# Two tiles of x loaded, rounded and split in halves instead of whole, in the first pass of a hybrid attention and gMLP block

## The chip, the cores and the metric

The kernel runs on one core of one Trainium2 chip. The metric is the device time of one execution in microseconds (us), as the median of several runs. The engines are TensorE (PE, the matmuls), VectorE (DVE), ScalarE (ACT), GpSimd (POOL) and SyncE (SP, whose queue issues most DMA transfers). Each engine runs its own instructions in a fixed order and waits on semaphores for what it needs from the others. Of the granted clock that the profile lists for TensorE, 1.00 is full speed.

## What is computed

One layer of an encoder block for 1024 tokens of width 1024, in float32. All projections of the normalised stream share one weight matrix.

```python
h = rmsnorm(x, norm_gain)
z = jnp.einsum('bsd,de->bse', h, w_in)
q, k, v, gate_a, u_in, v_in, gate_b, g_merge = jnp.split(z, IN_SPLITS, axis=-1)
...
q = axial_rope(rmsnorm(q.reshape(B, S, N_Q_HEADS, HEAD_DIM), q_gain), row_ang, col_ang)
k = axial_rope(rmsnorm(k.reshape(B, S, N_KV_HEADS, HEAD_DIM), k_gain), row_ang, col_ang)
attn = block_attention(q, k, v) * jax.nn.silu(gate_a)
y_a = jnp.einsum('bse,ed->bsd', attn, w_proj_attn)
...
v_mix = jnp.einsum('gij,bcjgd->bcigd', w_spatial, vv) + b_spatial.T[:, :, None]
gm = u * v_mix.reshape(B, S, GMLP_WIDTH) * jax.nn.silu(gate_b)
y_b = jnp.einsum('bse,ed->bsd', gm, w_proj_gmlp)
g = jax.nn.sigmoid(g_merge.reshape(B, S, N_BRANCHES, D_MODEL) + b_merge)
y = g[:, :, 0, :] * y_a + g[:, :, 1, :] * y_b
return x + jnp.einsum('bsd,de->bse', y, w_out)
```

There are 8 query heads on 2 key and value heads of 64, and a final RMS norm behind the layer.

## The kernel before

**Numbers in two parts.** To keep float32 accuracy with faster matmuls, an operand is split into a rounded high part and a low part, the rest. A product is then three matmuls (`mm3`, L173 to L176): high by high (L174), high by low of the second operand (L175), low by high (L176). The high part of x is made on ACT with the norm gain as a scale (`xh`, L158), the low part on DVE from the raw tile and the high part (`xl`, L159). Weights get theirs in `split` (high L112, low L118).

**The first pass.** x comes in transposed, in 8 tiles (dt = 0 to 7) of 128 channels by 1024 tokens, each 512 KB. `load_x(dt)` cuts a tile along the tokens: it issues one DMA for each cut on SP's queue (L152), then one ACT and one DVE instruction for each. For dt = 0 there are three cuts (256, 256 and 512 tokens), for all others one of 1024. `first_w` (L144) brings the first key and value weights in two pieces of 256 columns between those of dt 0; the later ones come by `stream_w` in pieces of 128 by 512, each for two dt (the first of them, for dt 2 and 3, is `wh_175`, `wl_176` in the order). For each dt, 24 matmuls of 128 x 256 go into the two key and value accumulators `kv_89` (tokens 0 to 511) and `kv_90` (tokens 512 to 1023), eight token blocks of three. The scheduler puts some of `kv_90`'s L174 and L175 ahead of `kv_89`'s first L176.

**Then** follow the gate and value projections from natural weights (`nat_weights`, `nat_group`), keys, queries, and from about 140 us attention. There, `scores` makes one tile of scores s (L552, L553), its row-maximum nm on DVE (L555), the exponential P on ACT (L559), the normalised high part of p on ACT (L565) and the low part on DVE (L566), and then transposes p by DMA on SP's queue (L569). `mix` multiplies the transposed T with the values (o, L577); ACT copies half of o (L580) and DVE adds it into `og` (L584). Between the heads stand matmuls of the gates and of u (`ga`, `u`; `fill_a`, `fill_u`, L490 to L492), whose results DVE takes out of PSUM (`ga01w`, L496; `uw`, L513). Query tiles are rotated on DVE (`qst`, `qtmp`: L317 to L332), transposed on PE (`qtp`, L351) and copied by ACT (`qT`, L353).

**The g stage**, from about 450 us: the merge gates are made by seven products of sub-matrices. The weights of each (`graw`) get a common scale: ACT sums their squares (`gsq`, L820), PE adds up (`usg`, L675), ACT copies (`scg`, L677), POOL makes the scale (L678, L679), and ACT writes scaled weights (`wg`, L686), which the first matmul g (L174) reads. `xf`, `xfT`, `gk`, `gf`, `gfT` are high parts of the other operands (L112) and `y` copies out of PSUM (L639), all on ACT.

**What sets the order.** No order is written by hand. The framework's scheduler (L1039, with a simulated timeline) places every instruction of every engine by its own estimate of when its inputs are ready. An edit at the start therefore also changes the order far behind it. SP has eight DMA semaphores: each DMA issue waits for the eighth before it.

Of the kernel before, what the change touches and what calls it, by code (L numbers as in the profile page):

```python
# [30 lines left out]
def hybrid_block_kernel(  # L31
# [21 lines left out]
    def t4(tag, name, dt=F32, shape=(P, 1024)):  # L53
        return sb.tile(list(shape), dt, tag=tag, bufs=BUFS[tag], name=name)
# [28 lines left out]
    def H(h):  # L83
        return slice(512 * h, 512 * h + 512)

    def C(c):
        return slice(128 * c, 128 * c + 128)
# [55 lines left out]
    def first_w(j):  # L143
        nc.sync.dma_start(out=wr[:, 256 * j:256 * j + 256], in_=wall[W_KV, :, 256 * j:256 * j + 256])  # L144

    def load_x(dt):
        raw = t4("T16", f"xraw{dt}")
        hi = t4("xh", f"xh{dt}", F32R)
        lo = t4("xl", f"xl{dt}", F32R)
        cuts = [slice(0, 256), slice(256, 512), H(1)] if dt == 0 else [slice(0, 1024)]  # L150
        for i, r in enumerate(cuts):
            nc.sync.dma_start(out=raw[:, r], in_=xT[C(dt), r])  # L152
            if dt == 0 and i == 0:
                nc.scalar.dma_start(out=cs, in_=cst[:, 0:C_BSP])
            if dt == 0 and i != 1:
                first_w(i // 2)
        for r in cuts:
            act.activation(hi[:, r], raw[:, r], AF.Copy, scale=gain[:, dt:dt + 1])  # L158
            dve.scalar_tensor_tensor(out=lo[:, r], in0=raw[:, r], scalar=gain[:, dt:dt + 1], in1=hi[:, r].bitcast(F32),  # L159
                                     op0=ALU.mult, op1=ALU.subtract)  # L160
        xh.append(hi)
        xl.append(lo)
        return raw
# [16 lines left out]
    for i in range(4):  # L180
        for j in range(2):
            dt = 2 * i + j
            if dt == 0:
                wh = sb.tile([P, 512], F32R, tag="wh", bufs=3, name="whk0")
                wl = sb.tile([P, 512], F32R, tag="wl", bufs=3, name="wlk0")
                wr = sb.tile([P, 512], F32, tag="wraw", bufs=4, name="wrawk0")
            raw = load_x(dt)
            if i == 0:
                r = slice(256 * j, 256 * j + 256)
                split(wh[:, r], wl[:, r], wr[:, r], act)  # L190
            elif j == 0:
                wh, wl = stream_w(W_KV + i // 2, i % 2, act)
            r = slice(256 * j, 256 * j + 256)
            for tt in range(NT):
                o = kvb[tt // 2][:, 256 * (tt % 2):256 * (tt % 2) + 256]
                mm3(o, xh[dt][:, C(tt)], xl[dt][:, C(tt)], wh[:, r], wl[:, r],
                    dt == 0 and tt % 2 == 0, dt == 7 and tt % 2 == 1)
# [845 lines left out]
```

## Time and profile before

| | us |
|---|---|
| median of 3 runs | 745.79 (744.92 to 745.86) |
| the profiled execution | 745.8 |
| its span in the trace | 744.0 |
| PE busy | 716.9 (96%) |
| DVE busy | 595.9 (80%) |
| ACT busy | 446.2 (60%) |
| mean granted clock of PE | 0.988 |

Lines of the profile name a source line (L158), an engine, an operation and its tiles, output first (`xh<-xraw,cs`). Numbers behind tile names, as in `xh_136`, count allocations; since the change allocates more tiles, they differ by 3 to 6 between the two kernels for the same thing (`wh_175` before is `wh_181` now, `xh_168` is `xh_171`). Times in the trace are from the start of the span. In brackets at a row's end stands how long the engine idled before it, and what ended that.

### The profile page before, as it was taken

How to read it: one execution, taken by the hardware profiler on the slowest of the kernel's cores; microseconds unless marked ns; L12 is line 12 of the kernel's file. 1: busy time of each engine (PE TensorE's matmuls, PEld its weight loads, DVE VectorE, ACT ScalarE, POOL GpSimd, SP SyncE). 2: the span in 40 equal slices, each digit the busy share in tenths (PEclk: the TensorE clock that was granted, in tenths of full speed). 3: DMA queues.
4: the chain of work that ended last, by engine and by line, in shares of the span. 5: the costliest groups of instructions: out<-in, count | busy, mean ns of one | idle time of the engine just before them, and what ended most of it. 6: DMA issues, size and time to landing. Idle time of an engine off the chain costs nothing.

```text
span 744.0 us, 9918 instructions
## 1 busy us (share of the span) xinstructions
PE 716.9 (96%) x3609; PEld 536.4 (72%) x3609; DVE 595.9 (80%) x900; ACT 446.2 (60%) x783; POOL 105.5 (14%) x101
## 2 busy tenths in 40 slices
PE   8999999988899999999999996999999999999996
PEld 7978888767778888888877883555464556478885
DVE  5567988799898999988899999988887898962223
ACT  5645665576788898877787477655455446531011
POOL 0010232123122322232200002101101110000000
PEclk9999999999999999999999997999999999999999
DMA  8831301064769898898999800130031004440202
GB/s 312 296 100 36 114 15 42 1 117 96 139 129 169 175 175 144 156 180 160 162 231 330 180 26 1 56 128 15 3 139 57 0 1 156 160 166 1 113 29 85
DMA packets 152609, 85.47 MB, mean 115 GB/s; under 512 B 135408, under 2 KB 136048, under 8 KB 152560
## 3 DMA queue, kind: packets, MB, share of 16 engines
q1 hardware_dynamic: 152272, 84.56, 45.6%
q8 instruction: 28, 0.46, 0.2%
q10 hardware_dynamic: 288, 0.28, 0.1%
q14 instruction: 21, 0.17, 0.1%
HBM read 47.07 MB, written 4.19 MB: 69 GB/s over the span
## 4 chain that ended last, share of the span: by engine, by line
PE 82%; DVE 6%; DMA 5%; ACT 3%; issue 2%; POOL 1%; SPq 0%; POOLq 0%; ACTq 0%; DVEq 0%
PE o L577 6%; DMA T<-p 4%; PE out L175 4%; PE out L176 4%; PE out L174 4%; PE g L174 3%; PE g L175 3%; PE g L176 3%; PE s L552 3%; PE s L553 3%; PE q L174 2%; PE q L176 2%; PE v L174 2%; PE v L175 2%; PE q L175 2%; PE v L176 2%
## 5 line engine op out<-in xcount | busy, mean ns | idle before, releaser
L566 DVE SCALAR_TENSOR_TENSOR p<-P,ri,p 128x1024 f16<-128x1024 f32 x64 | 88.9, 1394 | 14.4 <-ACT p L565 14.0
L559 ACT ACTIVATE P<-s,nm 128x1024 f32<-128x1024 f32 x64 | 71.4, 1116 | 22.5 <-DVE nm L555 11.2
L565 ACT ACTIVATE p<-P,ri 128x1024 f16<-128x1024 f32 x64 | 72.9, 1143 | 15.3 <-DMA T<-p 12.0
L555 DVE TENSOR_REDUCE nm<-s 128x1 f32<-128x1024 f32 x64 | 77.8, 1217 | 4.5 <-PE s L553 4.1
L577 PE MATMUL o<-T,vS 128*128 128x256 f16 x512 | 61.8, 273 | 2.1 <-DMA T<-p 2.1
L577 PEld LDWEIGHTS <-vS 128*128 128x128 f16 x512 | 47.4, 98 | 15.9 <-issue 6.3
L552 PE MATMUL s<-kT,qT 128*128 128x512 f32 x128 | 52.9, 414 | 1.3 <-ACT P L559 1.3
L118 POOL TENSOR_TENSOR wl<-wraw,wh 128x512 fp32r<-128x512 f32 x24 | 36.0, 1504 | 110.2 <-ACT wh L112 94.7
L553 PE MATMUL s<-kT,qT 128*128 128x512 f32 x128 | 50.5, 395 | 0.0
L973 DVE TENSOR_TENSOR xr<-out,xr 128x1024 f32<-128x1024 f32 x7 | 8.6, 1225 | 47.9 <-PE out L176 47.8
L915 ACT ACTIVATE sq<-xr 128x1024 f32<-128x1024 f32 x7 | 7.4, 1062 | 65.4 <-DVE xr L973 65.4
L678 POOL TENSOR_SCALAR scg<-scg 128x1 f32<-128x1 f32 x8 | 5.4, 674 | 216.5 <-ACT scg L677 216.5
L112 ACT CAST wh<-wraw 128x512 fp32r<-128x512 f32 x35 | 21.5, 614 | 19.3 <-PE yb L175 7.5
L490 PE MATMUL ga<-xh,wh 128*128 128x512 f32 x64 | 26.0, 407 | 3.8 <-DVE uw L513 3.4
L552 PEld LDWEIGHTS s<-kT,qT 128*128 128x128 f32 x128 | 24.1, 188 | 6.7 <-ACT P L559 1.8
L553 PEld LDWEIGHTS s<-kT,qT 128*128 128x128 f32 x128 | 24.1, 188 | 4.9 <-issue 0.2
L686 ACT ACTIVATE wg<-graw,scg 128x512 f16<-128x512 f32 x16 | 11.4, 721 | 26.1 <-PE g L176 13.1
L490 PE MATMUL u<-xh,wh 128*128 128x512 f32 x64 | 25.5, 399 | 0.7 <-DVE ga01w L496 0.7
L492 PE MATMUL ga<-xh,wl 128*128 128x512 f32 x64 | 25.6, 400 | 0.0
L491 PE MATMUL ga<-xl,wh 128*128 128x512 f32 x64 | 25.5, 399 | 0.0
L176 PE MATMUL yb<-gmh,wl 128*128 128x512 f32 x64 | 25.5, 398 | 0.0
L174 PE MATMUL yb<-gmh,wh 128*128 128x512 f32 x64 | 25.2, 396 | 0.3 <-ACT gmh L112 0.3
(558 smaller groups left out, 2188.3 us busy)
## 6 DMA issues: line engine op xcount, KB each, us to landing
wraw<-in_wall_dram SPq DMA_DIRECT2D x59, 256.0 KB, 3.2
graw<-in_wall_dram SPq DMA_DIRECT2D x16, 512.0 KB, 4.5
xraw<-in_xT_dram SPq DMA_DIRECT2D x15, 512.0 KB, 7.8
xn<-in_x_dram SPq DMA_DIRECT2D x8, 512.0 KB, 6.6
wor<-in_wall_dram SPq DMA_DIRECT2D x8, 512.0 KB, 5.5
xr<-in_x_dram SPq DMA_DIRECT2D x8, 512.0 KB, 4.1
out_dram<-xr SPq DMA_DIRECT2D x7, 512.0 KB, 2.6
T<-p SPq DMA_TRANSPOSE x64, 4.7
```

The lines of the kernel that those rows point to most:

```text
L118: eng_lo.tensor_tensor(out=lo, in0=raw, in1=hi if hi.dtype == F16 else hi.bitcast(F32), op=ALU.subtract)
L174: pe.matmul(o, ah, bh, start=start, stop=False)
L175: pe.matmul(o, ah, bl, start=False, stop=False)
L176: pe.matmul(o, al, bh, start=False, stop=stop)
L490: pe.matmul(o, wh[:, C(dt % 4)], xh[dt][:, H(h)], start=(dt == 0), stop=False)
L552: pe.matmul(sp[:, H(hf)], qs, kT[:, 2 * v, H(hf)], start=True, stop=False)
L553: pe.matmul(sp[:, H(hf)], qs, kT[:, 2 * v + 1, H(hf)], start=False, stop=True)
L555: dve.tensor_reduce(out=nm, in_=sp, axis=AX.X, op=ALU.max, negate=True)
L559: act.activation(Pt, sp, AF.Exp, bias=nm, accum_out=rsum)
L565: act.activation(hi, Pt, AF.Copy, scale=ri)
L566: dve.scalar_tensor_tensor(out=lo, in0=Pt, scalar=ri, in1=hi, op0=ALU.mult, op1=ALU.subtract)
L577: pe.matmul(ot[:, 0:256], vS[:, kt, v, :], T[:, :, 8 * p + kt, :], start=(kt == 0 and p == 0), stop=(kt == 7 and p == 1))
```

## The change

dt 1 and dt 2 are cut in two halves of 512 tokens. `H(0)` and `H(1)` are the column slices 0 to 511 and 512 to 1023.

```diff
-        cuts = [slice(0, 256), slice(256, 512), H(1)] if dt == 0 else [slice(0, 1024)]
+        cuts = [slice(0, 256), slice(256, 512), H(1)] if dt == 0 else [H(0), H(1)] if dt < 3 else [slice(0, 1024)]
         for i, r in enumerate(cuts):
             nc.sync.dma_start(out=raw[:, r], in_=xT[C(dt), r])
...
         for r in cuts:
             act.activation(hi[:, r], raw[:, r], AF.Copy, scale=gain[:, dt:dt + 1])
             dve.scalar_tensor_tensor(out=lo[:, r], in0=raw[:, r], scalar=gain[:, dt:dt + 1], in1=hi[:, r].bitcast(F32),
                                      op0=ALU.mult, op1=ALU.subtract)
```

So each of the two tiles has two DMAs of 256 KB, two ACT and two DVE instructions of 128 x 512 where it had one of each. On SP, the halves of dt 1 and dt 2 stand one behind the other where the whole tiles stood, and dt 4's tile has moved ahead of two weight pieces. On PE, all matmuls of dt 0 and dt 1 keep their order, and the first changes stand at dt 4.

**VectorE at the start**, from the last low part of the first weights on (`xl_137` belongs to dt 1, `xl_169` and now `xl_172` to dt 2, `wl_176` and `wl_182` to the weights of dt 2 and 3; `gsc` and `gs` are small scales that no matmul of this pass reads). Before:

```order
L118 TENSOR_TENSOR wlk_92<-wrawk_93,whk_91 128x256
L240 TENSOR_SCALAR gsc<-ssx 128x1
L242 RECIPROCAL gsc<-gsc 128x1
L243 TENSOR_SCALAR gs<-cs,gsc 128x8
L159 SCALAR_TENSOR_TENSOR xl_137<-xraw_135,cs,xh_136 128x1024
L159 SCALAR_TENSOR_TENSOR xl_169<-xraw_167,cs,xh_168 128x1024
L118 TENSOR_TENSOR wl_176<-wraw_173,wh_175 128x512
L159 SCALAR_TENSOR_TENSOR xl_205<-xraw_203,cs,xh_204 128x1024
```

With the change:

```order
L118 TENSOR_TENSOR wlk_92<-wrawk_93,whk_91 128x256
L159 SCALAR_TENSOR_TENSOR xl_137<-xraw_135,cs,xh_136 128x512
L240 TENSOR_SCALAR gsc<-ssx 128x1
L159 SCALAR_TENSOR_TENSOR xl_137<-xraw_135,cs,xh_136 128x512
L242 RECIPROCAL gsc<-gsc 128x1
L159 SCALAR_TENSOR_TENSOR xl_172<-xraw_170,cs,xh_171 128x512
L243 TENSOR_SCALAR gs<-cs,gsc 128x8
L159 SCALAR_TENSOR_TENSOR xl_172<-xraw_170,cs,xh_171 128x512
L118 TENSOR_TENSOR wl_182<-wraw_179,wh_181 128x512
L159 SCALAR_TENSOR_TENSOR xl_211<-xraw_209,cs,xh_210 128x1024
```

The three small instructions stood ahead of the low parts; now they stand between the halves.

**VectorE in attention**, at about 174 to 187 us of the profile. `p_1620`, `p_1637` are the low parts of two heads, now `p_1626`, `p_1643`; `nm_1669` and `nm_1686` are row-maxima of the next two, now `nm_1675`, `nm_1692`. Before:

```order
L317 TENSOR_TENSOR qst_1373<-qst_1373,qf_1778 128x1024
L555 TENSOR_REDUCE nm_1669<-s_1664 128x1
L328 TENSOR_TENSOR qtmp_1776<-qst_1373,tabq 128x16x16 x4
L566 SCALAR_TENSOR_TENSOR p_1620<-P_1614,ri_1617,p_1620 128x1024
L562 RECIPROCAL ri_1634<-ri_1634 128x1
L331 TENSOR_TENSOR qst_1373<-qst_1373,tabq 128x1024
L584 TENSOR_TENSOR og_1661<-o_1699,o_1716 64x128 x2
L555 TENSOR_REDUCE nm_1686<-s_1681 128x1
L332 TENSOR_TENSOR qst_1373<-qst_1373,qtmp_1776 128x1024
L566 SCALAR_TENSOR_TENSOR p_1637<-P_1631,ri_1634,p_1637 128x1024
L562 RECIPROCAL ri_1674<-ri_1674 128x1
L496 TENSOR_TENSOR ga01w<-ga_2147,rB 128x512
```

With the change:

```order
L317 TENSOR_TENSOR qst_1379<-qst_1379,qf_1784 128x1024
L566 SCALAR_TENSOR_TENSOR p_1626<-P_1620,ri_1623,p_1626 128x1024
L328 TENSOR_TENSOR qtmp_1782<-qst_1379,tabq 128x16x16 x4
L562 RECIPROCAL ri_1640<-ri_1640 128x1
L555 TENSOR_REDUCE nm_1675<-s_1670 128x1
L331 TENSOR_TENSOR qst_1379<-qst_1379,tabq 128x1024
L566 SCALAR_TENSOR_TENSOR p_1643<-P_1637,ri_1640,p_1643 128x1024
L332 TENSOR_TENSOR qst_1379<-qst_1379,qtmp_1782 128x1024
L555 TENSOR_REDUCE nm_1692<-s_1687 128x1
L584 TENSOR_TENSOR og_1667<-o_1705,o_1722 64x128 x2
L562 RECIPROCAL ri_1680<-ri_1680 128x1
L496 TENSOR_TENSOR ga01w<-ga_2153,rB 128x512
```

The first p stands ahead of a row-maximum and the four qtmp now, the second ahead of L332, a row-maximum and the og pair, and the `ga01w` behind them has the same instructions ahead of it. On PE, near the same place, 18 matmuls of `ga` (15 of `ga_2147`, now `ga_2153`, and three of dt 5) have moved ahead of the four matmuls of the s that `nm_1669` reads. On ACT, a P and a p now stand between the first and the second pair of the next qT copies.

**ScalarE ahead of the first g matmul**, at about 449 to 456 us (`scg` is the copy on which POOL's scale and then `wg` wait). Before:

```order
L639 COPY y_4203<-yb_4548 128x1024
L112 CAST gk<-gat_3891 128x1024
L820 ACTIVATE gsq_4738,gss_4737<-graw_4734 128x512
L677 COPY scg_4597<-usg_4592 128x1
L112 CAST gf_4925<-gat_3891 128x1024
L112 CAST xfT_4270<-xraw_4210 128x512
L820 ACTIVATE gsq_4740,gss_4737<-graw_4734 128x512
L686 ACTIVATE wg_4611<-graw_4580,scg_4597 128x512
```

With the change:

```order
L112 CAST xfT_4276<-xraw_4218 128x512
L112 CAST gf_4931<-gat_3897 128x1024
L820 ACTIVATE gsq_4746,gss_4743<-graw_4740 128x512
L639 COPY y_4209<-yb_4554 128x1024
L112 CAST gk<-gat_3897 128x1024
L112 CAST xfT_4276<-xraw_4216 128x512
L677 COPY scg_4603<-usg_4598 128x1
L820 ACTIVATE gsq_4748,gss_4743<-graw_4740 128x512
L820 ACTIVATE gsq_4750,gss_4743<-graw_4740 128x512
L686 ACTIVATE wg_4617<-graw_4586,scg_4603 128x512
```

`gf`, one `xfT` and one `gsq` have moved from behind the L677 to ahead of it. One `xf` cast has moved ahead of the last L580 copy before this place, and on PE the o matmuls that this copy reads stand five matmuls earlier.

## The prediction

> **What bounds the kernel now.** I read the page first, its busy shares and its chain.
>
> ```profile
> span 744.0 us, 9918 instructions
> PE 716.9 (96%) x3609; PEld 536.4 (72%) x3609; DVE 595.9 (80%) x900; ACT 446.2 (60%) x783; POOL 105.5 (14%) x101
> ...
> PE 82%; DVE 6%; DMA 5%; ACT 3%; issue 2%; POOL 1%; SPq 0%; POOLq 0%; ACTq 0%; DVEq 0%
> ```
>
> TensorE (PE) is busy 96% of the span and makes 82% of the chain. Work on another engine is free unless PE waits for it, so an edit can only win or lose inside PE's waits, 744.0 − 716.9 = 27 us with the head and the tail. The list of PE's waits says where they are (waited for, then total, times, longest).
>
> ```profile
> PE g L174 <- ACT wg L686: 6.6, 1, 6.6
> PE ga L490 <- DVE uw L513: 3.4, 1, 3.4
> PE o L577 <- DMA T<-p: 2.1, 3, 1.4
> PE kv L174 <- ACT xh L158: 2.0, 1, 2.0
> PE qtp L351 <- ACT qT L353: 1.3, 1, 1.3
> PE u L490 <- DVE ga01w L496: 0.7, 1, 0.7
> PE kv L176 <- DVE xl L159: 0.6, 1, 0.6
> ```
>
> The two kv rows belong to the edited place. The chain of waits from 3 us on, and the granted clock by microsecond, show what they cost (window, length, busy time and count of PE, PEld, DVE, ACT, POOL, then PEclk, DMA share, GB/s).
>
> ```profile
> 3.05 6.40 DMA xraw<-in_xT_dram
> 9.48 1.16 ACT xh L158
> 10.66 1.29 DVE xl L159
> 12.00 0.47 PE kv L176
> ...
> 13.11 0.21 PE kv L174
> ...
> 15.92 0.12 PE kv L175
> ```
>
> ```profile
> 8.00:9.00 1.00, 0.70 (x6) 0.50 (x5) 0.29 (x2) 0.00 (x0) 0.47 (x1) 1.00 1.01 385
> ...
> 13.00:14.00 1.00, 1.00 (x7) 1.00 (x7) 0.91 (x3) 1.00 (x2) 0.00 (x0) 0.50 1.05 410
> ```
>
> The second tile of x (dt = 1) is one 512 KB load. It lands at 3.05 + 6.40 = 9.45. Its rounding on ScalarE (ACT) and its low part on VectorE (DVE) follow one behind the other, and TensorE's first L176 of dt = 1 starts at 12.00. From there a matmul comes every 0.21 us, at a granted clock of 0.50, and only at 15.9 every 0.12 us again. So the place costs two waits (2.0 + 0.6) and a slow stretch: 20 of dt 1's 24 matmuls lie behind 12.00, and 20 × 0.12 = 2.4 would have done where they took from 12.00 to 15.99, 1.6 us more. The trace shows no cause for the low clock but these waits.
>
> **Part A, the start.** Moved and added: two loads of 512 KB become four of 256 KB, two ACT and two DVE instructions become four each; no matmul changes.
>
> ```profile
> xraw<-in_xT_dram SPq DMA_DIRECT2D x1, 256.0 KB, 3.5
> DMA to landing us min/median/max: 3.4/3.8/4.3
> ```
> ```profile
> 6.36 0.75 DVE L159 SCALAR_TENSOR_TENSOR xl<-xraw,cs,xh 128x512 fp32r<-128x512 f32 x1 [0.38 <-ACT xh L158]
> ...
> 13.15 0.68 DVE L118 TENSOR_TENSOR wl<-wraw,wh 128x512 fp32r<-128x512 f32 x1
> ```
> ```profile
> 3.75 0.51 ACT L158 ACTIVATE xh<-xraw,cs 128x256 fp32r<-128x256 f32 x1 [1.10 <-DMA cs<-in_cst_dram]
> ...
> 4.95 1.37 ACT L158 ACTIVATE xh<-xraw,cs 128x256 fp32r<-128x256 f32 x2
> 11.82 0.60 ACT L112 CAST wh<-wraw 128x512 fp32r<-128x512 f32 x1
> ```
> ```profile
> 15.99 0.40 PE L174 MATMUL kv<-wh,xh 128*128 128x256 f32 x2
> ```
>
> Landing of the first half: the DMA engines are full from 8 us on, at 385 to 410 GB/s, so 256 KB take 0.65 us. Earliest: right behind the last piece in front of it, the second half of the first weights (issued at 2.58, landing 4.3 later, 6.9), that is 7.5. Latest: with the second half, 9.45. I take 8.8, 0.65 before the landing that the trace shows, the nearest row. ACT's half costs 0.60 (the cast of 128x512) to 0.86 (1.37 for a 256 and a 512 piece, less 0.51 for the 256); I take 0.7: 9.5. DVE's half costs 0.75: 10.3. TensorE's third matmul of dt 1 reads the second half (landed 9.45, rounded 10.2), so its first L176 comes at 10.35, not 12.00. At full clock the 20 matmuls end at 12.75; the second low part, at 11.1, is ready before they reach it.
>
> Then the low part of dt 2's weights decides. DVE's queue is now: half, L240, half, L242, half, L243, half, L118. The dt 2 halves start at about 11.2 and 12.0 and end at 12.85 (dt 2's tile lands 1.3 behind dt 1's, at 10.75, its second half is rounded by 11.5, and the weights' cast of 0.60 behind it ends by 12.2); the L118 (0.68) ends at 13.5. So the first L175 of dt 2 comes at 13.55. Before, two L174 start at 15.99 and 16.11 and the L175 at 16.23. **Gain 2.7 us**. Ends: 3.2 if TensorE sets the pace (12.75 + 0.24 = 13.0); 1.6 if the clock still drops (10.35 + 20 × 0.21 = 14.55, and 0.24); 0.9 if the halves land together and the clock drops.
>
> Two more issues stand on SP's queue, 0.47 us each, in front of every later load; the full DMA engines, not the issue, set those landings, so I cost them nothing. If that cover were gone, TensorE would come 2.7 early to a load that is 0.94 late, and A would be +0.9 in place of −2.7.
>
> Whether the gain lasts is read from the stretch behind.
>
> ```profile
> 16.00:142.00 126.00, 126.00 (x683) 108.00 (x682) 96.02 (x171) 74.98 (x125) 22.28 (x15) 1.00 0.29 98
> ```
> ```profile
> 168.59 1.23 DVE L555 TENSOR_REDUCE nm<-s 128x1 f32<-128x1024 f32 x1 [1.88 <-PE s L553]
> ```
>
> TensorE has no wait between 16 and 142 us, and DVE still waits for PE behind the busy stretch, at 168.59, so the chain moves up as a whole.
>
> Two rules of the Trainium skill speak here. "TensorE: Matmul & The Clock Gate", Part 1 (the HAM clock gate), says that the clock halves after an idle window of about 3.4 us; this trace shows half clock after waits of 2.0 and 0.6 with four matmuls between, so a literal reading of single gaps does not hold here, and by it the 1.6 us would not have been lost. "DMA: Bandwidth & Descriptors", in Anatomy of one DMA, gives each transfer a fixed 2.0 us, and in Bandwidth advises batches of 1 MiB: it speaks against the change; were the fixed part paid one after another, two more transfers would bring dt 2's last half 4 us later, and the time to about 746, an estimate from that page. No row here shows transfers of the full queue paying it in turn, since 385 to 410 GB/s leaves no gap; it is rival 4.
>
> **Part B, attention from 163 to 200 us.** The order is made anew, and from here instructions stand elsewhere on PE, ACT and DVE.
>
> ```profile
> 184.76 1.91 PE L577 MATMUL o<-T,vS 128*128 128x256 f16 x16 [1.45 <-DMA T<-p]
> 187.36 0.50 PE L490 MATMUL u<-xh,wh 128*128 128x512 f32 x1 [0.69 <-DVE ga01w L496]
> ...
> 194.80 0.54 PE L351 MATMUL qtp<-identr,qs 128*128 128x128 f32 x4 [1.31 <-ACT qT L353]
> ```
> ```profile
> 176.63 2.53 DVE L328 TENSOR_TENSOR qtmp<-qst,tabq 128x256 f32<-128x256 f32 x4
> 179.08 1.27 DVE L566 SCALAR_TENSOR_TENSOR p<-P,ri,p 128x1024 f16<-128x1024 f32 x1
> ...
> 186.64 0.67 DVE L496 TENSOR_TENSOR ga01w<-ga,rB 128x512 f32<-128x512 f32 x1
> ```
> ```profile
> 192.97 1.15 ACT L565 ACTIVATE p<-P,ri 128x1024 f16<-128x1024 f32 x1 [1.49 <-DMA T<-p]
> ```
>
> DVE's p (L566, 179.08) now stands ahead of one row-maximum (1.14) and the four qtmp (2.45), so its transpose is issued up to 3.6 us earlier and the wait of 1.45 goes. But DVE waits for nothing between 174 and 192 (of its waits from 166 to 192 the list holds two row-maxima, the last at 172.4), and the same instructions stand before its ga01w as ever, which TensorE's u waits for: the 1.45 comes back in front of u. I count 0 for this pair (ends +0.7 and −2.1). The next p also stands earlier (ahead of og, a row-maximum and L332, 2.9 us), so its transpose frees the p buffer earlier, ACT's L565 loses its wait of 1.49, and the qT copies behind it release TensorE's qtp: **−1.3**. Other rows moved further on, where PE's waits are small; 0, with −1.3 and +4.1 as ends (the latter below).
>
> **Part C, the g stage.** TensorE waits 6.6 us for ACT's wg, behind L677 and POOL.
>
> ```profile
> 452.17 1.04 ACT L112 CAST gf<-gat 128x1024 fp32r<-128x1024 f32 x1
> 453.12 0.62 ACT L112 CAST xfT<-xraw 128x512 f16<-128x512 f32 x1
> 453.64 0.60 ACT L820 ACTIVATE gsq<-graw 128x512 f32<-128x512 f32 x1
> ```
> ```profile
> 440.86 0.37 ACT L580 COPY o<-o 64x256 f32<-64x256 f32 x1 [2.80 <-PE o L577]
> ```
>
> These three stood behind L677 and now stand ahead of it, 0.95 + 0.52 + 0.62 = 2.1 us; one xf cast of 0.52 went ahead of the copy at 440.86, which waits for PE. So ACT has 1.6 more between that copy and L677. The o matmuls that the copy waits for stand five matmuls of 0.23 earlier on PE, 1.2. **+0.4** (ends: −1.2 if the three go where ACT idles, +1.6 if the earlier o does not count).
>
> **Sum**: −2.7 − 1.3 + 0.4 = −3.6. The profiled execution took 745.8 (span 744.0 and 1.8 around it), the median of the runs is 745.79, so no correction: **742.2 us**.
>
> **Rivals.**
> 1. *The halves do not come early.* For it: two pieces in one full queue can share the engines, and the 6.40 us from issue to landing is no price of one load alone but of the queue. Against it: the loads in the trace land one after another. A gives 0.9, B's 1.3 comes back, since the second pair of qT copies now stands behind a P and a p on ACT (about 1.1 each), C +0.4: 745.3, within 0.2% (1.5 us, about what a measurement of this kernel can tell from no change). Chance 0.23.
> 2. *Slower: s of the next heads comes too late.*
>
> ```profile
> 162.63 0.23 PE ga L491
> ```
>
> In attention 18 matmuls of ga (18 × 0.23 = 4.1 us) now stand ahead of the second s tile on PE; from it follow row-maximum, exponential, p, transpose and o. DVE now has 3.6 us of other work (p, qtmp) ahead of that row-maximum, less 0.3 that it waited, so by the rows the s is there in time. If ACT or the transposes fall behind, up to 4.1 us come back as a wait: −2.7 + 4.1 + 0.4 = +1.8, and with 0.3 of slowed clock 747.9. It decides as soon as new waits exceed 2.3 us. The waits of 3.4 (ga on uw) and 6.6 in this kernel show that such ones exist. Chance 0.15.
> 3. *More goes*: A 3.2, and of B the u wait too (−3.4 in all), C +0.4: 739.6. Chance 0.14.
> 4. *Each transfer pays for itself in turn.* A 256 KB piece lands 3.5 after its issue, 0.65 of it moving data. Were the other 2.85 paid in turn, two more transfers would put dt 2's second half 5.7 later, at 16.45, rounded at 17.15 where TensorE read it at 16.1: A +1.0, so 745.9. Against it stand the full engines. Chance 0.03.
>
> **How the numbers follow.** Forecast 0.45, which spans 740.6 to 744.2. Faster by over 0.2%: 0.45 + 0.14 = 0.59; within 0.2%: 0.23 + 0.03 = 0.26; slower: 0.15. The range 739.6 to 747.6 leaves out about half of rival 2 and half of rival 3, and a little beyond.
>
> **What would show it.** Right in A: the two kv waits under 1 us together, no microsecond from 10 to 16 below a clock of 0.9, first L175 of dt 2 near 13.5. Wrong in A: the first half lands after 9.2, or half clock in 12 to 15. B: no wait of o for T near 182, u's wait for ga01w near 2 us, no qtp wait. C: the wait for wg between 5.4 and 8.2. What makes the forecast wrong is a new wait of over 2 us on PE between 160 and 380 us, or the 3.4 us wait for uw growing by what A gained, which would mean that DVE, not PE, sets the time there.

## The result and the profile after

| | before | with the change |
|---|---|---|
| median of the runs at the first comparison, us | 745.83 (744.92 to 746.01, 4 runs) | 740.20 (739.11 to 741.50, 4 runs) |
| profiled execution, us | 745.8 | 740.55 |
| span, us | 744.0 | 738.8 |
| ratio, 95% interval | | 0.9934 (0.9915 to 0.9954) |

The change makes the kernel faster by 0.66%, and 742.2 was forecast. Two later comparisons, with more executions, gave 0.9950 (0.9937 to 0.9962; 744.64 and 740.97) and 0.9957 (0.9940 to 0.9974; 744.98 and 741.39). So the gain is 3.6 us rather than 5.6, and the forecast was 3.6. That the sum fits is partly luck: two of its three terms are not what the forecast said, as the terms one by one show.

The busy shares, and the list of TensorE's waits, of the changed kernel (waited for, then total, times, longest):

```profile
span 738.8 us, 9919 instructions
PE 715.2 (97%) x3609; PEld 534.9 (72%) x3609; DVE 592.8 (80%) x902; ACT 447.4 (61%) x785; POOL 111.1 (15%) x101
```
```profile
PE usg L675 <- ACT gsq L820: 4.9, 1, 4.9
PE ga L490 <- DVE uw L513: 3.4, 1, 3.4
PE o L577 <- DVE og L584: 3.3, 3, 2.0
PE s L552 <- ACT P L559: 1.1, 2, 0.7
...
PE kv L174 <- ACT xh L158: 1.0, 1, 1.0
...
PE o L577 <- DMA T<-p: 0.2, 1, 0.2
```

The busy time of TensorE has hardly changed; the waits have. At the start 1.0 is left of 2.0 + 0.6. The 6.6 for wg has become a 4.9 for the squares of the next tile. The waits for ga01w and qtp have gone, 0.2 of those for T is left, and waits for og, 3.3 in all, have come. The start, in the timeline of ACT and PE (start, duration, then the idle time before in brackets) and in the granted clock (the third number from the end):

```profile
7.28 0.72 ACT L158 ACTIVATE xh<-xraw,cs 128x512 fp32r<-128x512 f32 x1 [0.55 <-DMA xraw<-in_xT_dram]
9.29 1.99 ACT L158 ACTIVATE xh<-xraw,cs 128x512 fp32r<-128x512 f32 x3 [1.28 <-DMA xraw<-in_xT_dram]
```
```profile
10.06 0.39 PE L174 MATMUL kv<-whk,xh 128*128 128x256 f32 x1 [0.99 <-ACT xh L158]
...
13.04 0.32 PE L175 MATMUL kv<-wl,xh 128*128 128x256 f32 x1
```
```profile
12.00:13.00 1.00, 1.00 (x11) 1.00 (x10) 0.92 (x2) 0.51 (x1) 0.00 (x0) 1.00 0.98 391
```

The halves of dt 1 land at 7.3 and 9.3, TensorE goes on at 10.06, the clock stays at 1.00, and the first L175 of dt 2 comes at 13.04, 3.2 earlier than the 16.23 of before.

To see where the gain lies, three places are read in both traces: the last L174 of the queries (at the end of the projections), the last L176 of yb (in front of the g stage) and the last L176 of the output. Rows of the views of the tiles q, yb and out; the first and last start stand behind the durations. Before:

```profile
L174 PE MATMUL q<-nh,xh x64: 387/389/481, 84.7 to 136.4; 128*128 128x512 f32 x64
...
L176 PE MATMUL yb<-gmh,wl x64: 387/396/481, 397.3 to 448.3; 128*128 128x512 f32 x64
...
L176 PE MATMUL out<-wo,yl x32: 389/390/399, 677.9 to 737.0; 128*128 128x512 f32 x32
```

With the change:

```profile
L174 PE MATMUL q<-nh,xh x64: 387/389/481, 81.5 to 133.2; 128*128 128x512 f32 x64
...
L176 PE MATMUL yb<-gmh,wl x64: 389/396/481, 393.6 to 444.6; 128*128 128x512 f32 x64
...
L176 PE MATMUL out<-wo,yl x32: 389/390/399, 672.6 to 731.7; 128*128 128x512 f32 x32
```

So between these two executions 3.2 were won before 136 us (A), 0.5 from there to the g stage (B: 311.9 became 311.4), and 1.6 behind it (C: 288.7 became 287.1). The forecast had 2.7, 1.3 and a loss of 0.4.

### The profile page after: what moved, and what is told of

Read it like the earlier page. It is cut to its first block, busy times and chain, and to the rows that moved or that the text cites. A ratio compares the mean times of both kernels' runs of the same rounds, so it can differ in the third digit from the quotient of the medians.

```text
span 738.8 us, 9919 instructions
## 1 busy us (share of the span) xinstructions
PE 715.2 (97%) x3609; PEld 534.9 (72%) x3609; DVE 592.8 (80%) x902; ACT 447.4 (61%) x785; POOL 111.1 (15%) x101
## 4 chain that ended last, share of the span: by engine, by line
PE 65%; DVE 14%; DMA 11%; ACT 6%; issue 3%; SPq 0%; POOL 0%; POOLq 0%; ACTq 0%; DVEq 0%
DMA T<-p 10%; DVE p L566 4%; PE out L175 4%; PE out L176 4%; PE out L174 4%; PE o L577 3%; PE g L174 3%; PE g L176 3%; PE g L175 3%; DVE nm L555 3%; ACT p L565 2%; PE q L174 2%; PE q L176 2%; PE v L175 2%; PE v L174 2%
## 5 line engine op out<-in xcount | busy, mean ns | idle before, releaser
L566 DVE SCALAR_TENSOR_TENSOR p<-P,ri,p 128x1024 f16<-128x1024 f32 x64 | 84.3, 1321 | 16.5 <-ACT p L565 16.3
L118 POOL TENSOR_TENSOR wl<-wraw,wh 128x512 fp32r<-128x512 f32 x24 | 39.7, 1655 | 111.0 <-ACT wh L112 68.8
L678 POOL TENSOR_SCALAR scg<-scg 128x1 f32<-128x1 f32 x8 | 5.0, 626 | 209.6 <-ACT scg L677 209.6
L686 ACT ACTIVATE wg<-graw,scg 128x512 f16<-128x512 f32 x16 | 11.4, 721 | 25.5 <-PE g L176 13.1
L175 PE MATMUL v<-nl,xh 128*128 128x512 f32 x64 | 25.4, 397 | 0.0
L176 PE MATMUL v<-nh,xl 128*128 128x512 f32 x64 | 25.4, 396 | 0.0
```

Source lines behind the costliest of these rows:

```text
L118: eng_lo.tensor_tensor(out=lo, in0=raw, in1=hi if hi.dtype == F16 else hi.bitcast(F32), op=ALU.subtract)
L175: pe.matmul(o, ah, bl, start=False, stop=False)
L176: pe.matmul(o, al, bh, start=False, stop=stop)
L566: dve.scalar_tensor_tensor(out=lo, in0=Pt, scalar=ri, in1=hi, op0=ALU.mult, op1=ALU.subtract)
```

## The experiments

Theory 1: at the start, dt 1's halves let ACT, DVE and TensorE work one behind the other, which cuts the wait. Theory 2: the half clock comes from TensorE's idle time. Theory 3: POOL's part in C stands still while DVE works without a gap. Theory 4: only a part of the gain is the start, the rest is the new order. The rivals stand with each run. All ratios are against the kernel before, run beside it on the same chip.

**One part of the change at a time.** Four kernels, each shown against the changed one. Only dt 1:

```diff
-        cuts = [slice(0, 256), slice(256, 512), H(1)] if dt == 0 else [H(0), H(1)] if dt < 3 else [slice(0, 1024)]
+        cuts = [slice(0, 256), slice(256, 512), H(1)] if dt == 0 else [H(0), H(1)] if dt == 1 else [slice(0, 1024)]
```

> Only dt 1 comes in halves, dt 2 whole. Theory 1 (dt 1 is what counts: its halves pass ACT, DVE and TensorE one behind the other, the wait in front of dt 1 shrinks to about 1 us and the clock does not drop): TensorE reaches dt 2 as early as with the change (first matmul of dt 2 near 12.8) and then waits up to 0.7 us for the low part of dt 2's weights behind the whole xl; at dt 3 it is 2.4 to 3.2 us ahead of the kernel before. Rival (both halvings are needed): less than 1.6 us ahead. The order behind 160 us is new again, so the total may differ from this by 2 us: 741 to 744 by theory 1.

Only dt 2:

```diff
-        cuts = [slice(0, 256), slice(256, 512), H(1)] if dt == 0 else [H(0), H(1)] if dt < 3 else [slice(0, 1024)]
+        cuts = [slice(0, 256), slice(256, 512), H(1)] if dt == 0 else [H(0), H(1)] if dt == 2 else [slice(0, 1024)]
```

> Only dt 2 comes in halves. Order behind as in the kernel before but for a few rows. Theory 1: the wait in front of dt 1 (2.0 and 0.6) and the half clock stay, TensorE reaches dt 2 at 16.0 and finds it ready: 745.8, within 0.7. Rival (the split of dt 2 is what counts): 1 us or more below.

Halves in the computing, one DMA for each tile:

```diff
-        for i, r in enumerate(cuts):
+        for i, r in enumerate([slice(0, 1024)] if dt in (1, 2) else cuts):
             nc.sync.dma_start(out=raw[:, r], in_=xT[C(dt), r])
```

> dt 1 and dt 2 each by one DMA of 512 KB, but rounded and split in halves. PE order as in the kernel before. Theory 1: dt 1 lands at 9.45 as before, first L176 near 11.0; if the clock holds, TensorE is 2.0 to 2.6 us ahead at dt 3 and the total is 743.5; if it still drops, 1.0 ahead and 744.8. Rival (the early landing of the first half makes the gain): less than 0.5 ahead, 745.5.

Two DMAs for each tile, computing on whole tiles:

```diff
-        for r in cuts:
+        for r in [slice(0, 1024)] if dt in (1, 2) else cuts:
             act.activation(hi[:, r], raw[:, r], AF.Copy, scale=gain[:, dt:dt + 1])
```

> dt 1 and dt 2 each by two DMAs of 256 KB, but rounded and split whole. Theory 1: ACT waits for the second half, which lands at about 9.3, and nothing else is gained: 0 to 0.3 us ahead at dt 3, half clock stays, 745.6. Rival (the early landing makes the gain): 2 us or more ahead. If each transfer pays for itself in turn: behind the kernel before by up to 1 us.

Measured, with the kernel before and the changed one beside them (places of the last query, yb and output matmul as above; "again" is the same kernel in a later chip run). The medians of the kernel before differ by chip run: 743.98 for the first four experiments, 744.98 for the second run of halves in computing, and for the change as told above; so the ratios are what compares. They are not quotients of these medians, and differ from them by up to 0.1%.

| kernel | median, us | ratio, 95% | queries | yb | output |
|---|---|---|---|---|---|
| before | 743.98 to 745.83 | | 136.4 | 448.3 | 737.0 |
| dt 1 alone | 742.45 | 0.9970 (0.9957 to 0.9982) | 133.7 | 445.7 | 733.3 |
| dt 2 alone | 744.96 | 1.0005 (0.9991 to 1.0018) | 135.6 | 449.4 | 737.8 |
| halves in computing | 743.03 | 0.9994 (0.9980 to 1.0008) | 133.6 | 445.5 | 733.9 |
| again | 743.43 | 0.9986 (0.9973 to 0.9999) | 133.7 | 447.3 | 735.6 |
| halves in DMA | 746.26 | 1.0030 (1.0016 to 1.0045) | 134.7 | 447.8 | 736.2 |
| the change | 740.20 | 0.9934 (0.9915 to 0.9954) | 133.2 | 444.6 | 731.7 |
| again | 740.97 | 0.9950 (0.9937 to 0.9962) | 133.9 | 447.3 | 734.3 |
| again | 741.39 | 0.9957 (0.9940 to 0.9974) | 133.0 | 443.0 | 730.0 |

For the start theory 1 holds. In all nine traces of kernels with dt 1 computed in halves (the fills below included), the queries end at 132.8 to 133.9, with one transfer or with two; in the five with dt 1 whole, at 134.1 to 136.4. So the early landing of the first half is not what does it: TensorE's third matmul of dt 1 reads the second half anyway.

Split transfers alone made the kernel slower by 0.3%, for a cause that stays open. The trace does not put it at the start: the queries end 1.7 earlier than in the trace of before, and the half clock, which was expected to stay, is not there. What the ten executions do show is a lower mean clock, 0.9868 against 0.9887 for the kernel before. By an estimate from these two (0.0019 x 744) that is 1.4 of the 2.3 us between the medians.

Another expectation failed badly. With halves in the computing, whose order on TensorE is that of the kernel before, the trace ended 3.1 earlier, and yet the median is only 0.95 and 1.55 below, and the ratios say 0.06 and 0.14%, the first with an interval that holds 1. A single pair of traces does not tell what the start is worth.

**What the start of the kernel before costs, in several executions.** The kernel without L678 (below) has the start of the kernel before, unchanged. Its first wait, in the timeline of PE, and its clock:

```profile
9.96 0.39 PE L174 MATMUL kv<-whk,xh 128*128 128x256 f32 x1 [1.11 <-ACT xh L158]
```
```profile
12.00:13.00 1.00, 1.00 (x11) 1.00 (x10) 1.00 (x2) 0.95 (x1) 0.00 (x0) 1.00 1.06 422
```
```profile
L174 PE MATMUL q<-nh,xh x64: 389/389/481, 82.5 to 134.1; 128*128 128x512 f32 x64
```

The same instructions waited 1.1 where the profiled execution of before waited 2.0, the clock stayed at 1.00, and the queries ended at 134.1, not 136.4. So the 3.2 between the first two traces holds 2.3 that the kernel before wins by itself in another execution. The times of 81 executions of the kernel before in the later chip runs fit that: 31 had a mean granted clock of 0.990 or more, with a median of 743.37, and 50 had less, with 745.25. They do not say in which place the clock fell.

**Is it the idle time?** The kernel before, with 16 matmuls that nobody reads:

```diff
+            for _ in range(16 if dt == 0 else 0):
+                pe.matmul(warmp[:, 0:256], xl[0][:, C(7)], wh[:, 0:256], start=True, stop=True)
```

> The kernel before, with 16 matmuls whose results nobody reads between those of dt 0 and dt 1, which fill TensorE from 8.7 to about 10.6 us. Data, loads and the two waits' ends are as before. Theory 2 (the clock falls because TensorE is idle): no half clock at 12 to 16, the first L176 of dt 1 at 12.0 as before, dt 1 ends at 14.4 instead of 16.0, TensorE 1.6 us ahead at dt 3. Rival (the low clock has another cause, such as the loads or a fixed time after the start): half clock at 12 to 16 remains, 0 ahead. The order behind 160 us is new, so the total says less: 742 to 746.

The timeline of PE, the clock, and the two longest waits (lines behind L198 stand two lower in this kernel):

```profile
8.74 2.08 PE L199 MATMUL warmp<-whk,xl 128*128 128x256 f32 x16
...
12.06 0.39 PE L176 MATMUL kv<-whk,xl 128*128 128x256 f32 x1 [0.58 <-DVE xl L159]
```
```profile
12.00:13.00 1.00, 0.94 (x8) 0.94 (x8) 1.00 (x2) 0.71 (x2) 0.00 (x0) 1.00 1.03 418
```
```profile
PE g L174 <- ACT wg L688: 9.6, 1, 9.6
PE yb L174 <- ACT P L561: 4.9, 1, 4.9
```

The first L176 comes at 12.06 as before, and the clock does not fall; the queries end at 135.1, 1.3 earlier than in the trace of before. One such trace proves less than it seems, since the start without the fill has kept its clock too. In the five starts with whole tiles the idle times of 2.0 + 0.6 (before) and 1.7 + 0.6 (dt 2 alone) were followed by half clock, 1.2 + 0.6 (halves in DMA), 1.1 + 0.6 (without L678) and the filled 0.6 were not, and none of the nine starts with dt 1 in halves has a clock below 1.00 there.

A line between long and short waits does not follow from this. Behind the wait of 3.4 for uw, which all traces have, 13 show half clock and one (the first of the fills at the g stage, below) shows none; behind the wait of 2.0 to 2.1 for og this same trace and the second of the change show it, and the first of the change does not. So theory 2 is borne out where a wait was filled without half clock to follow (here and in the g stage, below), and which wait brings half clock in a given execution stays open.

The total of this kernel was 760.01, ratio 1.0212 (1.0197 to 1.0228), where 742 to 746 was expected. Sixteen matmuls at 9 us have changed the order some 400 us later: TensorE now waits 4.9 for P and 9.6 for wg. **A new order, and the half clock behind its waits, can cost this kernel 2%**, which is more than any term of the forecast.

**The change again, beside it halves in the computing.** The same kernel twice more, and on the second of these chip runs the kernel with halves in the computing beside it:

> The changed kernel once more, beside the kernel before on the same chip and in more executions. If the half-clock stretch at 12 us is there in only some of the executions of the kernel before (its times there spread from 741.3 to 746.3 with mean clocks from 0.984 to 0.992), the gain is smaller in the middle than between the two traces: 0.4 to 0.6%, and the executions of the kernel before with the highest clocks are 1.5 to 2 us below the others. If the stretch is always there: 0.7%.

> Halves in the computing alone, one transfer per tile, with the order of the kernel before: once more, on the same chip as the changed kernel. Theory 4 (the start is worth about 1 us in the middle of many executions, since the half clock at 12 us and part of the wait are there only in some executions of the kernel before; the rest of the gain is the new order): 0.5 to 1.5 us below the kernel before, and about 2 us or more above the changed kernel. Rival (the start makes the whole gain): equal to the changed kernel within 0.7 us.

> The changed kernel, for the comparison with the run before this one: 3 to 4 us below the kernel before.

Medians 740.97; then 743.43 and 741.39, with 744.98 for the kernel before. So of 3.6 us, 1.5 come with halves in the computing in the old order (1.0 by the ratio), and 2.0 more only with the change itself, as theory 4 has it. The rival, that the start makes the whole gain, falls. The two kernels differ in the order and in the transfers; no run has the new order with whole transfers, so that it is the order is read from where the time is won, which is behind the start.

From the last yb to the last output, the rows of the table leave little doubt on C: 288.7, 288.4, 288.4, 288.3 and 288.4 in the five traces with (nearly) the old order, 287.1, 287.0 and 287.0 in the three of the change. C is a gain of 1.4; dt 1 alone, whose order is new too, has 287.6. From the queries to yb it is 311.9 to 313.8 in those five and 311.4, 313.4 and 310.0 in these three, so B is about 1.3 in the mean, with a spread as large. The same matmuls lie between these places in both kernels, so TensorE's idle time there can be compared: 9.4, 9.4 and 9.7 (before, and twice halves in computing) against 9.0, 8.2 and 7.9 with the change, 1.1 less in the mean. Two of the changed kernel's own traces show what makes the spread (windows from 160 us on; the granted clock is the third number from the end). The first trace:

```profile
160.00:164.00 4.00, 4.00 (x26) 3.25 (x26) 3.56 (x7) 1.93 (x6) 0.45 (x1) 1.00 0.99 136
```

The second:

```profile
160.00:164.00 4.00, 4.00 (x12) 3.08 (x11) 4.00 (x7) 1.95 (x5) 0.00 (x0) 0.61 0.89 92
```

Behind the wait for uw the clock was low until 159.5 in the one and until 163.5 in the other: 12 matmuls in four microseconds instead of 26. The second has half clock behind the wait for og as well. All traces with the old order that have the short stretch behind uw (before, halves in computing, without L678) take 311.9 for B.

**POOL in the g stage.** The kernel before without L678:

```diff
-        act.copy(sc[:, 1:2], pt[:, 0:1])
-        pool.tensor_scalar(out=sc[:, 1:2], in0=sc[:, 1:2], scalar1=1.0, scalar2=1e-30, op0=ALU.mult, op1=ALU.add)
+        act.activation(sc[:, 1:2], pt[:, 0:1], AF.Copy, bias=1e-30)
```

> The kernel before, with L678 (POOL) left out and its small constant added by ACT in L677; same order elsewhere. In the trace of before L678, on 128 numbers, lasted from 452.37 to 455.38, when DVE's unbroken run of instructions from 451.70 ended at 455.33. Theory 3 (POOL stands still while DVE works without a gap): POOL's next one, L679, now starts near 452.4 and ends only at the end of DVE's run, near 455.4, so wg comes 0.6 us earlier and no more. Rival (L678 is long by itself or by waking POOL up): if by itself, wg comes 3 us earlier, 743; if by waking up, L679 takes 3 us wherever DVE's run ends.

Ratio 0.9994 (0.9981 to 1.0006). Timelines of POOL and DVE. The kernel before:

```profile
452.37 3.01 POOL L678 TENSOR_SCALAR scg<-scg 128x1 f32<-128x1 f32 x1 [76.69 <-ACT scg L677]
455.46 0.56 POOL L679 TENSOR_TENSOR scg<-scg,mhalf 128x1 f32<-128x1 f32 x1
```
```profile
454.64 0.69 DVE L118 TENSOR_TENSOR xfT<-xraw,xfT 128x512 f16<-128x512 f32 x1
```

Without L678:

```profile
450.12 3.38 POOL L679 TENSOR_TENSOR scg<-scg,mhalf 128x1 f32<-128x1 f32 x1 [76.66 <-ACT scg L677]
```
```profile
452.40 0.69 DVE L118 TENSOR_TENSOR xfT<-xraw,xfT 128x512 f16<-128x512 f32 x1
```

With the change:

```profile
449.42 0.64 POOL L678 TENSOR_SCALAR scg<-scg 128x1 f32<-128x1 f32 x1 [73.90 <-ACT scg L677]
```
```profile
448.78 1.23 DVE L118 TENSOR_TENSOR gk<-gat,gk 128x1024 fp32r<-128x1024 f32 x1 [0.65 <-ACT gk L112]
```

L678 is an instruction on 128 numbers. In the kernel before it ended at 455.38, when DVE's run had ended at 455.33. Taken out, the next one lasted 3.38 and ended at 453.50, 0.41 behind the end of DVE's run at 453.09. So it is not the instruction that is long, and the rival "long by itself" falls: from L677 to wg it took 0.3 less, 0.6 were expected. With the change it ended at 450.06, right behind DVE's gk at 450.01. There POOL had idled for 73.90 before, about as long as the 76.69 of before, so waking up is not it either.

Theory 3 fits all three, and other orders too. With 16 matmuls at the start L678 lasted 4.00 and ended at 468.03, where DVE's run ended at 467.98; with the fill in a bank of its own (below), 2.49, at 450.77 and 450.72. The Trainium skill, "SBUF — State Buffer", SBUF: two separate sides, says that of a DVE instruction with two SBUF inputs and a GpSimd instruction that reads SBUF, whichever starts first shuts the other out for its whole instruction; the traces agree that it is blocked, but in four of these five kernels for a run of several DVE instructions, not for one. Why POOL got its turn at the first seam of DVE in the changed kernel and at none of three in the kernel before stays open.

**Filling the wait of 4.9 us.** Three attempts at a better kernel, on top of the change. First, six matmuls into the bank of the first usg:

```diff
         act.copy(sc[:, 1:2], pt[:, 0:1])
+        for _ in range(6 if name == 'g0' else 0):
+            pe.matmul(pt[:, 128:512], mscale.broadcast_to([P, P]), ss[:, n - 1:n].broadcast_to([P, 384]), start=True, stop=True)
```

> The changed kernel, with six matmuls of 128 x 384 whose results nobody reads behind the first usg, in the wait of 4.9 us before the g stage; order elsewhere the same but for a few rows. Theory 2: TensorE is idle for about 1 us instead of 4.9, the clock does not fall at 449 to 456, the nine g matmuls that took 0.43 take 0.22 and the eight usg take half: 2 to 2.7 us less than the changed kernel in the same chip's runs. Rival: the clock falls anyway, 0 to 0.3 us.

It gave 742.03, ratio 0.9969 (0.9957 to 0.9980), 1.1 above the changed kernel. The matmuls waited 3.6 for L677, which reads another column of the same bank, so they did not fill the wait but stood in front of g, which began at 457.65. Then seven, in a bank of their own, and the same without L678:

```diff
+        if name == 'g0':
+            dum = ps_oz(len(nscale) + 1, 'dum')
+            for _ in range(7):
+                pe.matmul(dum, mscale.broadcast_to([P, P]), ss[:, n - 1:n].broadcast_to([P, 512]), start=True, stop=True)
```

> The changed kernel, with seven matmuls of 128 x 512 whose results nobody reads behind the first usg, now in a PSUM bank of their own, so that they wait for nothing but the sums of squares; the usg of the next tile has gone behind the first g matmuls. Order elsewhere as with the change but for some 30 rows. Theory 2: TensorE is busy from 445.9 to about 451, g starts near 451.9 as wg allows, the clock stays at 1.00, nine g matmuls take 0.22 instead of 0.43: 2 to 3 us below the changed kernel. Rival (the clock falls anyway, or the fill delays g): 0 or above.

> As the run before this one, and L678 left out with its small constant added in L677. L678 took 0.64 in the trace of the changed kernel: wg and g 0.3 to 0.8 us earlier than in the run before this one, if the fill ends before wg is there; nothing, if the fill of about 5 us ends later than wg.

Measured: 743.65, ratio 0.9982 (0.9972 to 0.9992), and 743.45, ratio 0.9983 (0.9971 to 0.9996): both 2 us above the changed kernel (741.39). The first of them, in the timeline, the windows and the waits (the trace has two rows for each of these seven matmuls):

```profile
445.91 6.28 PE L681 MATMUL dum<-gss,mscale 128*128 128x512 f32 x14
452.22 0.39 PE L174 MATMUL g<-xf,wg 128*128 128x512 f16 x1
```
```profile
453.00:457.00 4.00, 3.99 (x19) 1.67 (x18) 4.00 (x6) 3.91 (x11) 0.00 (x0) 1.00 0.02 6
```
```profile
PE g L174 <- DVE ga L706: 1.5, 1, 1.5
PE g0T L176 <- DVE wg0T L691: 1.4, 2, 1.1
```

Here theory 2 is right and worth nothing. The fill held the clock at 1.00, and g started in time. The same window of the changed kernel:

```profile
453.00:457.00 4.00, 4.00 (x13) 1.46 (x12) 4.00 (x7) 1.84 (x6) 3.20 (x5) 0.60 0.02 4
```

There the clock was 0.60, and 13 matmuls ran instead of 19. But new waits for ga and wg0T, behind an order that had moved once more, took all of it and 2 us on top; DVE, on which they wait, is busy all of these four microseconds in both kernels. Without L678 the next one again lasted long, 2.83. No version beat the changed kernel.

## Why the prediction was right or wrong

**What bounds the kernel** was read rightly: PE's busy time did not move, and all that was won was waits and half clock.

**A, forecast −2.7.** In the two profiled executions 3.2, from the causes that it names. The halves landed at 7.3 and 9.3, where 8.8 and 9.45 were taken; the first of these made no difference, since the second half sets the start of TensorE's third matmul of dt 1, and with it of the first L176 (forecast 10.35, measured 10.40). DVE did not set the pace at dt 2: it had finished wl before TensorE came, the better end of the range (in the second trace of the change TensorE waited 0.4 for it). One end of that range is added up wrongly: 16.23 − 14.55 − 0.24 is 1.4, not 1.6. What failed is the size for the median: I took one trace of before, in which the wait was at its longest of those seen and the clock had dropped, as what the kernel does. In another execution the same start is 2.3 better. Halves in the computing, in the old order, measured 0.95 and 1.55 in the median, 0.4 and 1.0 by the ratios.

**The two rules.** The rule that the prediction takes from the Trainium skill, half clock after an idle window of about 3.4 us, did not fit the trace gap by gap, as the prediction says, and one trace has a wait of 3.4 without half clock behind it. The Trainium skill's "TensorE: Matmul & The Clock Gate", Part 1, says in another sentence that the window runs free, so that one kernel gets different results. Executions of one kernel do differ here, in the clock at the same places; the window itself no run shows. The fixed 2.0 us that the prediction takes from the Trainium skill's "DMA: Bandwidth & Descriptors", Anatomy of one DMA, stands there for transfers that GpSimd issues, while x comes on SP's queue. Paid in turn (rival 4) it did not show: dt 1's two halves both landed before 9.45. That two transfers without split computing made the kernel slower by 0.3% speaks for the Trainium skill's advice of large batches, which the prediction quotes, only if the transfers are the cause, and that is not shown.

**B, forecast −1.3.** The waits moved almost as told: the wait of o for T is 0.2, and the qtp wait has gone. But the wait of u for ga01w, for which 1.45 was to come back, has gone too, because DVE's instructions ahead of ga01w did not cost the same as before. From L317 (`qst`) to ga01w DVE took 12.3 (174.35 to 186.64) and now takes 11.2 (170.57 to 181.81), since the second p lasted 2.30 beside a POOL instruction and now lasts 1.28. In the kernel before:

```profile
183.37 2.20 POOL L118 TENSOR_TENSOR wl<-wraw,wh 128x512 fp32r<-128x512 f32 x1 [5.49 <-ACT wh L112]
```
```profile
184.35 2.30 DVE L566 SCALAR_TENSOR_TENSOR p<-P,ri,p 128x1024 f16<-128x1024 f32 x1
```

With the change:

```profile
177.66 1.28 DVE L566 SCALAR_TENSOR_TENSOR p<-P,ri,p 128x1024 f16<-128x1024 f32 x1
```

Four traces with the old order have 2.29 or 2.30 there, the three of the change 1.27 or 1.28; that POOL held it up is argued from the rows, not tested. The prediction also names og as one of the rows that p has passed, and prices only what p gains. TensorE's o has a single PSUM buffer, which og sets free, so the next o waits 2.0 for og. 1.4 + 0.7 + 1.3 became 2.0. Together these come near the forecast by another way than the one it was added up from, and waits further on differ as well, so that the size fits the mean of the later traces is luck, with a spread from the clock as large as itself.

**C, forecast +0.4; measured −1.4.** The sign was wrong. ACT did get more to do ahead of L677, as told: from the copy of o at 436.06 to L677 at 449.18 it took 13.1, where it took 11.3 (440.86 to 452.13), and the copy came 1.2 earlier against the last yb. So the part that was added up came out at +0.7. The step that failed is the silent one: that POOL's L678 and L679 behind it cost the same as before. L678 took 0.64 instead of 3.01, as it met another place in DVE's run, and from L677 to the first wg it took 2.6 instead of 4.7; that outweighed the rest. The usg of the next tile then stood ahead of g on TensorE, as the timeline of PE shows, so that g began 0.7 behind the first wg (ready at about 451.8). In the profiled executions fewer of the g matmuls also fell into the half clock, which lasted until 456.5 with the change, 4 us from the start of g, and until 463 before, 6 us from it.

```profile
450.76 1.86 PE L675 MATMUL usg<-gss,mscale 128*128 128x1 f32 x8 [4.93 <-ACT gsq L820]
452.48 0.59 PE L174 MATMUL g<-xf,wg 128*128 128x512 f16 x1
```

**The rivals.** The halves come early, so rival 1 is out, though the start is worth about as little in the median as it said (0.9). Rival 2, the late s, did not come: no new wait on TensorE in attention reaches the 2.3 us that it needed; the longest is the 2.0 for og. That new orders make new waits was right as a danger, and not for this change: the fill at the start found one that costs 2%.

## What to carry to other kernels

Where a tile passes two engines on its way to a third, halve it for the computing when the third one waits, and measure whether the transfer has to be halved too; here it did not. Before pricing a stall from one trace, look at how far several executions of the same kernel differ there, above all where a half-clock stretch hangs on it. And where a scheduler makes the order, compare an edit with another one that keeps the order: some 2.0 of the 3.6 us here came behind the edited place, among instructions that the edit never named, and another harmless edit lost 15 in the same way.

## What the runs showed of the hardware

Half clock comes in stretches of one length. Added up over half-microsecond windows, each place with half clock between 8 and 490 us has 3.4 us of it or a whole multiple (6.8, 10.2, once 17.1), in all 14 traces. The number of stretches differs between executions of one kernel: behind the wait for uw the clock was low from 155.5 to 159.5 in one trace of the changed kernel (3.4 us in all) and from 156 to 163.5 in another (6.8). At a clock of 0.61 over the four microseconds from 160 on, this one stretch is worth 1.6 us by estimate (0.39 x 4), against the 3.6 that the change won.

A GpSimd instruction on 128 numbers can last 2.5 to 4 us beside a VectorE that works without a gap, until 0.05 behind the end of VectorE's run (3.01, 4.00 and 2.49 in three orders), and 0.64 in another order.
